# FFN output of a hybrid decoder block: 16 of its 22 contraction blocks as seven half-block products

## The chip, the cores and the metric

The kernel runs on one core of a Trainium2 chip. The metric is the device time of one execution in microseconds (us), median of the runs shown; lower is better. A separate profiled execution gives the trace. Engines are named as the profile names them: PE (TensorE matmuls), PEld (TensorE weight loads), DVE (VectorE), ACT (ScalarE), POOL (GpSimd) and SP (SyncE, which issues every DMA of this kernel).

## The reference, cut to what matters

One layer: an input projection, a Mamba-2 mixer and an RG-LRU mixer side by side, two output projections merged by gates, `w_out`, then the FFN that the change is about.

```python
h = h + (g_ssm * y_ssm + g_lru * y_lru) @ w_out[l]
hn = rmsnorm(h, norm2_w[l])
gate, up = jnp.split(hn @ w_ffn_in[l], 2, axis=-1)
h = h + (jax.nn.silu(gate) * up) @ w_ffn_out[l]
return rmsnorm(h, norm_f_w)
```

`h` is 1024 tokens by 1024 features; the FFN's hidden width is 2816 = 22 blocks of 128. All data is float32.

## The kernel before, in words

Everything is kept transposed: 128 features on the partitions, tokens along the free dimension, in two halves of 512 (`h`). A float32 operand is split into a high part `hi` (fp32r, a cast on ACT) and a low part `lo = x - hi` (a subtraction on DVE, with `x` and `hi` both in SBUF); `split`, lines 98 and 99. A product of two blocks is then three matmuls, hi·hi, lo·hi and hi·lo (lines 175 to 177 and 960 to 962). So each 128x128 weight block against 512 tokens costs three 128x512 matmuls, and each operand costs one ACT and one DVE instruction before it.

Stages in order: the input projection and the two mixers (to about 1000 us of the trace), the two mixer output projections, `w_out` (lines 965 to 1001), the FFN input (1008 to 1054), the FFN output (1057 to 1148). The tile framework places all semaphores and, from the order of the program and what is ready, the order on each engine; each engine runs its own queue in that order.

**The FFN input** already multiplies by halves. For a pair of column blocks (gate and up) and both token halves, the eight half-block products are replaced by seven, with sums of weight quarters made on POOL (`pair_sums`, four instructions of 512 columns) and sums of activation quarters made once, in the `w_out` stage (lines 988 to 999). One pair is 7 products of 12 matmuls, 84 matmuls; there are 22 pairs. The result of pair j is stored to the DRAM buffer `act_d[j]`.

**The FFN output** is direct: the 22 contraction blocks in four groups (`FFG`, of 6, 6, 5 and 5). For each of the first three groups the activations are loaded from `act_d` and split (`load_group`), and for each of 8 column tiles `d` and each token half a bank of PSUM collects the group's matmuls, and DVE adds it to `res` (line 1089). The last group runs over tokens 0 to 511, 512 to 767 and 768 to 1023, with the squares, the final norm and the stores of `out` folded in. Its weights come in through `last_w`, 512 columns at a time. At the change from the FFN input to the FFN output the pool `ar1` is closed and `ar2` and `res` are laid over its space.

PSUM has 8 banks of 512 columns (`pb`). SBUF tiles of two 512-column rows are "units", from the pools `ar0` (8) and `ar1` (29); `tp` has 13 tiles of 512 columns for short-lived values.

Of the kernel before, what the change touches and what calls it, by code (L numbers as in the profile page):

```python
# [60 lines left out]
NTMP = 13  # L61
NUNIT = 29

FFG = ((0, 6), (6, 12), (12, 17), (17, 22))
# [3 lines left out]
def hybrid_block(ctx, tc, xT, w_in, w_dt, w_os, w_ol, w_o, w_fi, w_fo, w_fl, lru_w, params, heads, out):  # L68
# [219 lines left out]
    with ExitStack() as st1:  # L288
# [470 lines left out]
        tp = ctx.enter_context(tc.tile_pool(name="tp", bufs=NTMP, reuse_waits="tile"))  # L759
# [3 lines left out]
        with tc.tile_pool(name="lru", bufs=1, reuse_waits="tile", side="right") as lp, tc.tile_pool(  # L763
# [66 lines left out]
            y0 = [act_pair(ar0, load_half(yn_d[i][:, hcol[0]])) for i in range(8)]  # L830
# [48 lines left out]
    yl = [load_acts(ar1, yl_d, h) for h in range(2)]  # L879
# [11 lines left out]
    for d in range(KD):  # L891
        mg[1][d] = act_pair(ar1, res[d][:, 1, :])
# [7 lines left out]

    raws, wops = {}, {}

    def pair_load(j):
        raws[j] = []
        for q in range(2):
            raw = wpool.tile([P, KD, P], F32, name="raw", tag="raw", bufs=2)
            load(raw, w_fi[q * NFF + j])
            raws[j].append(raw)

    def pair_a1(j):  # L910
        raw = raws[j][0]
        hi = wpool.tile([P, KD, P], F32R, name="whi", tag="whi")
        lo = wpool.tile([P, KD, P], F32R, name="wlo", tag="wlo")
        split(hi, lo, raw)
        wops[j] = {"a11": (hi[:, 0:4, :], lo[:, 0:4, :]), "a12": (hi[:, 4:8, :], lo[:, 4:8, :])}

    blk = lambda t_: t_.rearrange("p (k c) -> p k c", c=P)

    def pair_sums(j):

        g_, u_ = raws[j]
        s12, s34 = unit(ar1, F32, "s12"), unit(ar1, F32, "s34")
        s = [blk(t_[:, i, :]) for t_ in (s12, s34) for i in range(2)]
        G.tensor_tensor(s[0], u_[:, 0:4, :], u_[:, 4:8, :], op=ALU.add)
        G.tensor_tensor(s[1], s[0], g_[:, 0:4, :], op=ALU.add)
        G.tensor_tensor(s[2], g_[:, 0:4, :], u_[:, 0:4, :], op=ALU.add)
        G.tensor_tensor(s[3], s[1], g_[:, 4:8, :], op=ALU.add)
        wops[j]["s"] = s12, s34

    def pair_a22(j):  # L930
        u = unit(ar1, name="a22")
        hi, lo = blk(u[:, 0, :]), blk(u[:, 1, :])
        split(hi, lo, raws[j][1][:, 4:8, :])
        wops[j]["a22"] = hi, lo

    def pair_s(j, i):
        src = wops[j]["s"][i]
        hi, lo = unit(ar1, name="sh"), unit(ar1, name="sl")
        split(hi, lo, src)
        for q in range(2):  # L940
            wops[j][f"s{2 * i + q + 1}"] = blk(hi[:, q, :]), blk(lo[:, q, :])

    xop = {}

    def xop_put(name, k, pool, src, neg=False):

        if k % 2 == 0:
            xop.setdefault(name, []).append((unit(pool, name="xh"), unit(pool, name="xl")))
        hi, lo = (t_[:, k % 2, :] for t_ in xop[name][k // 2])
        if neg:  # L950
            S.activation(hi, src, AF.Copy, scale=-1.0)
            V.scalar_tensor_tensor(lo, src, -1.0, hi.bitcast(F32), op0=ALU.mult, op1=ALU.subtract)
        else:
            split(hi, lo, src)
# [12 lines left out]
    for h in range(2):
        for d in range(KD):
# [10 lines left out]
            sumsq(rs2[h], r, d == 0)  # L979
            k, kh = d % 4, d // 4  # L980
            if k % 2 == 0:
                bn[h, kh, k // 2] = unit(ar1, F32, "bn")
            b = lambda h_, kh_: bn[h_, kh_, k // 2][:, k % 2, :]
            S.activation(b(h, kh), r, AF.Copy, scale=pcol("n2", d))
            if h == 0:
                xop_put(("b11", "b21")[kh], k, ar1, b(h, kh))
            elif kh == 0:
                V.tensor_tensor(b(0, 0), b(1, 0), b(0, 0), op=ALU.subtract)
                xop_put("t1", k, ar1, b(0, 0))
            else:  # L990

                pool = ar0 if k < 2 else ar1
                V.tensor_tensor(b(0, 0), b(1, 1), b(0, 0), op=ALU.subtract)
                xop_put("t2", k, pool, b(0, 0))
                G.tensor_tensor(b(1, 0), b(1, 0), b(1, 1), op=ALU.subtract)
                V.tensor_tensor(b(0, 1), b(0, 1), b(0, 0), op=ALU.subtract)
                xop_put("t3", k, pool, b(1, 0))
                xop_put("t4", k, pool, b(0, 1))
                xop_put("n22", k, pool, b(1, 1), neg=True)
            if h == 1 and d == 0:  # L1000
                rms_scale(rs2[0], rs2[0], bank(), 1.0 / D, epst[:, 0:1])
    pair_sums(0)
    pair_s(0, 0)
    pair_a22(0)
    pair_s(0, 1)


    for j in range(NFF):
        wo = wops[j]
        last = j == NFF - 1  # L1010
        nxt = lambda f, *a: None if last else f(j + 1, *a)
        nxt(pair_load)
        px, pv, py, pz = bank(), bank(), None, None
        product(px, wo["a11"], "b11", True, False)
        s1 = temp("s1")
        S.copy(s1, px)
        if j == 0:
            product(px, wo["a12"], "b21", False, True)
            product(pv, wo["s1"], "t1", True, False)
        else:  # L1020
            product(pv, wo["s1"], "t1", True, False)
            product(px, wo["a12"], "b21", False, True)
        nxt(pair_a1)
        nxt(pair_sums)
        py = bank()
        product(py, wo["s2"], "t2", True, False)
        if j == 0:
            rms_scale(rs2[1], rs2[1], bank(), 1.0 / D, epst[:, 0:1])
        sg = temp("sg")
        V.tensor_tensor(sg, px, rs2[0], op=ALU.mult)  # L1030
        S.activation(sg, sg, AF.Silu)
        u2 = temp("u2")
        V.tensor_tensor(u2, s1, py, op=ALU.subtract)
        product(py, wo["s3"], "t3", False, True)
        nxt(pair_s, 0)
        V.tensor_tensor(s1, py, s1, op=ALU.subtract)
        su = temp("su")
        V.tensor_tensor(su, pv, s1, op=ALU.add)
        pz = bank()
        product(pz, wo["a22"], "t4", True, True)  # L1040
        nxt(pair_a22)
        V.tensor_tensor(s1, pz, s1, op=ALU.add)
        V.tensor_tensor(s1, s1, rs2[0], op=ALU.mult)
        V.tensor_tensor(sg, sg, s1, op=ALU.mult)
        store(act_d[j][:, hcol[0]], sg)
        product(pv, wo["s4"], "n22", False, True)
        nxt(pair_s, 1)
        V.tensor_tensor(u2, u2, pv, op=ALU.subtract)
        V.tensor_tensor(u2, u2, rs2[1], op=ALU.mult)
        S.activation(u2, u2, AF.Silu)  # L1050
        V.tensor_tensor(su, su, rs2[1], op=ALU.mult)
        V.tensor_tensor(u2, u2, su, op=ALU.mult)
        store(act_d[j][:, hcol[1]], u2)
        del wops[j], raws[j]
# [183 lines left out]
```

## Time and profile before

| what | value |
|---|---|
| three timed runs | 2108.53, 2112.59, 2111.17 us; median 2111.17 us |
| profiled execution | 2113.38 us, span of the trace 2111.4 us |
| PE busy | 2066.4 us, 9702 matmuls |
| DVE, ACT, POOL busy | 1261.3, 856.0, 406.7 us |
| granted TensorE clock, mean | 0.989 |
| DMA | 212.17 MB, 100 GB/s over the span |

Times in rows are microseconds from the start of the span unless marked ns. Matmuls are pipelined, so a matmul's own duration is longer than the distance from one to the next. "Idle before" is the time that an engine waited ahead of an instruction, with the instruction that ended the wait behind the arrow.

### The profile page before, as it was taken

To read this page: it belongs to the slowest core of one execution; us is meant where nothing else is said; L and a number is where in the kernel's file an instruction comes from. 1 tells how busy PE (TensorE), PEld (TensorE's weight loads), DVE (VectorE), ACT (ScalarE), POOL (GpSimd) and SP (SyncE) were. 2 spreads that over 40 slices of the span, in tenths; PEclk is the share of its full clock that TensorE was granted. 3 is DMA by queue.
4 is the path that set the end of the run, shared out by engine and by line. 5 is a ranking of instruction groups with operands and counts; after the bars stand their busy time and mean duration, and the time that the engine had idled before them with its cause. 6 is when DMAs were issued, how large, how long until landed. Compare 5 with 4: busy or idle time off the path is not lost.

```text
span 2111.4 us, 24842 instructions
## 1 busy us (share of the span) xinstructions
PE 2066.4 (98%) x9702; PEld 1681.2 (80%) x9702; DVE 1261.3 (60%) x1587; ACT 856.0 (41%) x1253; POOL 406.7 (19%) x378
## 2 busy tenths in 40 slices
PE   8999999999999999999999999988999999999998
PEld 6677887887887888888888888866888888878887
DVE  8655567567667546555514544588666666654336
ACT  5334445445455436666513221453223222233124
POOL 5103333334343410000000000234322332100000
PEclk8999999999999999999999999999999999999999
DMA  3222223323223243211314431542222222283122
GB/s 140 88 62 88 85 77 117 103 75 113 88 77 118 89 159 135 75 65 60 128 52 159 144 114 58 162 148 97 67 87 90 82 70 88 74 287 107 52 59 80
DMA packets 99973, 212.17 MB, mean 100 GB/s; under 512 B 11024, under 2 KB 29456, under 8 KB 99856
## 3 DMA queue, kind: packets, MB, share of 16 engines
q1 hardware_dynamic: 99856, 210.59, 30.9%
q8 instruction: 76, 1.25, 0.2%
q14 instruction: 41, 0.34, 0.1%
HBM read 168.34 MB, written 42.21 MB: 100 GB/s over the span
## 4 chain that ended last, share of the span: by engine, by line
PE 87%; DVE 5%; issue 2%; POOL 2%; ACT 2%; DMA 1%; SPq 0%; DVEq 0%; POOLq 0%; ACTq 0%
PE pj L175 12%; PE pj L177 11%; PE pj L176 11%; PE pbk L175 9%; PE pbk L177 9%; PE pbk L176 9%; PE pbk L960 6%; PE pbk L962 6%; PE pbk L961 6%; PE yb L661 1%; PE yb L649 1%; DVE xs L494 1%; PE tr L627 1%; DVE wlo L99 1%; DVE xl L332 1%
## 5 line engine op out<-in xcount | busy, mean ns | idle before, releaser
L175 PE MATMUL pj<-hnh,whi 128*128 128x512 f32 x1152 | 461.0, 400 | 0.0
L177 PE MATMUL pj<-hnl,whi 128*128 128x512 f32 x1152 | 452.8, 393 | 0.0
L176 PE MATMUL pj<-hnh,wlo 128*128 128x512 f32 x1152 | 451.7, 392 | 0.0
L177 PE MATMUL pbk<-un,whi 128*128 128x512 f32 x816 | 317.8, 390 | 1.3 <-DVE un L99 1.3
L175 PE MATMUL pbk<-un,whi 128*128 128x512 f32 x816 | 317.9, 390 | 1.0 <-ACT un L98 1.0
L176 PE MATMUL pbk<-un,wlo 128*128 128x512 f32 x816 | 317.3, 389 | 0.0
L98 ACT CAST whi<-raw 128x1024 fp32r<-128x1024 f32 (+3 forms) x172 | 167.2, 972 | 308.8 <-PE pbk L177 199.7
L99 DVE TENSOR_TENSOR wlo<-raw,whi 128x1024 fp32r<-128x1024 f32 (+3 forms) x172 | 201.5, 1172 | 142.8 <-ACT whi L98 140.9
L177 PEld LDWEIGHTS pj<-hnl,whi 128*128 128x128 f32 x1152 | 216.6, 188 | 48.1 <-issue 0.5
L175 PEld LDWEIGHTS pj<-hnh,whi 128*128 128x128 f32 x1152 | 216.7, 188 | 45.8 <-issue 2.4
L176 PEld LDWEIGHTS pj<-hnh,wlo 128*128 128x128 f32 x1152 | 216.9, 188 | 44.9 <-issue 1.4
L177 PEld LDWEIGHTS pbk<-un,whi 128*128 128x128 f32 x816 | 153.2, 188 | 35.2 <-DVE un L99 3.2
L175 PEld LDWEIGHTS pbk<-un,whi 128*128 128x128 f32 x816 | 153.2, 188 | 33.3 <-ACT un L98 1.7
L176 PEld LDWEIGHTS pbk<-un,wlo 128*128 128x128 f32 x816 | 153.2, 188 | 31.8 <-issue 0.2
L960 PE MATMUL pbk<-xh,sh 128*128 128x512 f32 x352 | 140.1, 399 | 13.2 <-ACT sh L98 10.0
L857 POOL TENSOR_TENSOR rs<-rs,sq 128x512 f32<-128x512 f32 x14 | 22.7, 1620 | 639.2 <-ACT sq L856 639.2
L961 PE MATMUL pbk<-xh,sl 128*128 128x512 f32 x352 | 137.3, 390 | 0.4 <-DVE sl L99 0.4
L962 PE MATMUL pbk<-xl,sh 128*128 128x512 f32 x352 | 137.3, 390 | 0.0
L620 ACT ACTIVATE E<-csb,cs 128x128 f32<-128x128 f32 x256 | 82.8, 392 | 107.6 <-PE yb L661 100.4
L98 ACT CAST sh<-s 128x1024 fp32r<-128x1024 f32 x44 | 46.3, 1052 | 171.3 <-PE pbk L961 157.8
L960 PEld LDWEIGHTS pbk<-xh,sh 128*128 128x128 f32 x352 | 66.1, 188 | 35.1 <-ACT sh L98 10.4
L1089 DVE TENSOR_TENSOR res<-res,pbk 128x512 f32<-128x512 f32 x48 | 32.8, 686 | 87.4 <-PE pbk L177 87.4
(265 smaller groups left out, 3366.3 us busy)
## 6 DMA issues: line engine op xcount, KB each, us to landing
raw<-in_w_in SPq DMA_DIRECT2D x74, 512.0 KB, 3.5
raw<-in_w_fi SPq DMA_DIRECT2D x44, 512.0 KB, 3.9
csb<-cs_d SPq DMA_DIRECT2D x64, 256.0 KB, 3.5
ld<-act_d SPq DMA_DIRECT2D x44, 256.0 KB, 5.4
yn_d<-xs SPq DMA_DIRECT2D x16, 512.0 KB, 3.2
ld<-yn_d SPq DMA_DIRECT2D x32, 256.0 KB, 5.2
raw<-in_w_os SPq DMA_DIRECT2D x16, 512.0 KB, 3.5
gt<-gate_d SPq DMA_DIRECT2D x32, 256.0 KB, 4.1
```

Of the source, the lines that this page charges most:

```text
L98: S.copy(hi, src)
L99: V.tensor_tensor(lo, src, hi.bitcast(F32), op=ALU.subtract)
L175: PE.matmul(ps, wh, xh, start=i == 0, stop=False)
L176: PE.matmul(ps, wl, xh, start=False, stop=False)
L177: PE.matmul(ps, wh, xl, start=False, stop=i == n - 1)
L332: V.scalar_tensor_tensor(lo, x, pcol("n1", k), hi.bitcast(F32), op0=ALU.mult, op1=ALU.subtract)
L620: S.activation(E[:, j, :], csb[:, j, :], AF.Relu, bias=cs[:, c, h0 + j : h0 + j + 1], scale=-1.0)
L857: G.tensor_tensor(acc, acc, sq, op=ALU.add)
L960: PE.matmul(ps, wh, xh, start=first and k == 0, stop=False, skip_group_check=True)
L961: PE.matmul(ps, wl, xh, start=False, stop=False, skip_group_check=True)
L962: PE.matmul(ps, wh, xl, start=False, stop=last and k == 3, skip_group_check=True)
L1089: V.tensor_tensor(r, r, ps, op=ALU.add)
```

## The change

The FFN output takes contraction blocks 0 to 15 in two parts of 8 (`NPART`), each by halves: the 8 blocks as two halves of 4 in the contraction, column tiles in pairs (p, p + 4) for p = 0 to 3, tokens in two halves. Eight half-block products become seven (`NQ`), each 4 blocks deep, 12 matmuls. It runs product by product over the four pairs of column tiles: 28 steps ("slots") of 12 matmuls in each part. Blocks 16 to 21 stay direct, in the last group (6 blocks in place of 5). A table of events, `at(slot, f, ...)`, says at which slot the loads, the sums and the splits are issued: loads 10 to 12 slots ahead, a weight split three slots ahead (`LAW`), an activation split in the four slots of the product before. The events ahead of slot 0 are issued between the products of the last FFN input pair (`lead`, `pump`).

The sums: weights, four POOL instructions for each p and part (`w_sum`); activations, one on DVE and three on POOL for each k of 0 to 3 and part (`x_diff`). Results go to `res` through one instruction a product (ACT for product 0, DVE reading PSUM for the others), and three POOL additions for each p and part.

The memory is laid out anew: `ar` has 22 units, `br` 6 (for `res`, `bn`, `c0`, `c1`, then `res` of the end), `sp1` five tiles of 512 columns, `wq` five units laid over `tp` when that is closed after the `w_out` stage; `tp` has 10 tiles. The FFN input keeps its seven products, but its operand sums are taken otherwise: the weight sums overwrite the raw weights in place, the activation sums (`t_parts`) are four DVE instructions and two splits of 1024 columns for each k, and the second token half of `w_out` runs over column tiles 4, 5, 6, 7, 0, 1, 2, 3. The stores of `out` go one column tile at a time, 24 in place of 12.

```diff
-NTMP = 13
-NUNIT = 29
-FFG = ((0, 6), (6, 12), (12, 17), (17, 22))
+NTMP = 10
+NUNIT = 22
+NPART = 2
+NLAST = NFF - 8 * NPART
...
+    wo_order = [list(range(KD)), [4, 5, 6, 7, 0, 1, 2, 3]]
+    wseq += [(w_o[d], KD) for h in range(2) for d in wo_order[h]]
...
+    def pair_sums(n):
+        g_, u_ = raws[n]
+        s1 = sp1.tile([P, H], F32, name="ws1", tag="ws1")
+        wops[n]["raw1"] = s1
+        G.tensor_tensor(blk(s1), u_[:, 0:4, :], u_[:, 4:8, :], op=ALU.add)
+        G.tensor_tensor(u_[:, 0:4, :], u_[:, 0:4, :], g_[:, 0:4, :], op=ALU.add)
+        G.tensor_tensor(g_[:, 0:4, :], g_[:, 0:4, :], blk(s1), op=ALU.add)
+        G.tensor_tensor(g_[:, 4:8, :], g_[:, 4:8, :], g_[:, 0:4, :], op=ALU.add)
...
+    def t_parts(x, k, u1, u2, pool):
+        V.tensor_tensor(u1[:, 0, :], u1[:, 0, :], u1[:, 1, :], op=ALU.subtract)
+        V.tensor_tensor(u1[:, 1, :], u1[:, 1, :], u2[:, 1, :], op=ALU.subtract)
+        V.tensor_tensor(u2[:, 1, :], u2[:, 1, :], u1[:, 0, :], op=ALU.add)
+        V.tensor_tensor(u2[:, 0, :], u2[:, 0, :], u2[:, 1, :], op=ALU.subtract)
+        for u, names in ((u1, ("t1", "t3")), (u2, ("t4", "t2"))):
+            hi, lo = unit(pool, name="xth"), unit(pool, name="xtl")
+            split(row(hi), row(lo), row(u))
...
-            if h == 1 and d == KD - 1:
+            if h == 1 and i == KD - 2:
                 pair_load(0)
-                pair_a1(0)
             ps = bank()
             mm_act(ps, w, mg[h])
+            if h == 1 and i == KD - 1:
+                pair_a1(0)
+                pair_sums(0)
+                pair_s1(0)
...
+    def first_pair():
+        product(px, wo["a11"], x["b11"], True, False)
+        S.copy(c1[:, 0, :], px)
+        product(px, wo["a12"], x["b21"], False, True)
+        product(pv, wo["s4"], x["b22"], True, True)
+        pair_s(0, 1)
...
+    LAW = 3
+    def x_part(i, n, k):
+        u1, u2 = xu[i, k], xu[i, k + 4]
+        src = (u1[:, 0], u2[:, 0], u1[:, 0], u2[:, 1], u2[:, 1], u1[:, 1], u2[:, 0])[n]
+        xop.setdefault((i, n), []).append(act_pair(ar, src))
+    def x_diff(i, k, n):
+        u1, u2 = xu[i, k], xu[i, k + 4]
+        if n == 0:
+            V.tensor_tensor(u1[:, 0], u1[:, 0], u1[:, 1], op=ALU.subtract)
+        elif n == 1:
+            G.tensor_tensor(u1[:, 1], u1[:, 1], u2[:, 1], op=ALU.subtract)
...
+    def w_sum(i, p, n):
+        g_, u_ = wr[i, p, 0], wr[i, p, 1]
+        if n == 0:
+            ws1[i, p] = blk(sp1.tile([P, H], F32, name="ws1", tag="ws1"))
+            G.tensor_tensor(ws1[i, p], u_[:, 0:4], u_[:, 4:8], op=ALU.add)
+        elif n == 1:
+            G.tensor_tensor(u_[:, 0:4], u_[:, 0:4], g_[:, 0:4], op=ALU.add)
+            G.tensor_tensor(g_[:, 0:4], g_[:, 0:4], ws1[i, p], op=ALU.add)
+        else:
+            G.tensor_tensor(g_[:, 4:8], g_[:, 4:8], g_[:, 0:4], op=ALU.add)
+    def w_part(i, n, p):
...
+        t_ = wpool.tile([P, 2, 4, P], F32R, name="wop", tag="whi" if (n * NP + p) % 2 else "wlo")
+        split(t_[:, 0], t_[:, 1], src)
...
+        for p in range(NP):
+            at(s0 - 12 + p, load_w, i, p, 0)
+            at(s0 - 6 + p, load_w, i, p, 1)
+            at(s0 - 10 + p, load_x, i, p)
+            at(s0 - 7 + p, load_x, i, p + 4)
+            at(s0 + p, w_sum, i, p, 0)
+            at(s0 + 3 + p, w_sum, i, p, 1)
+            at(s0 + 4 + p, w_sum, i, p, 2)
+            for n in range(NQ):
+                at(s0 + (n - 1) * NP + p, x_part, i, n, p)
+                at(s0 + n * NP + p - LAW, w_part, i, n, p)
+            at(s0 + 2 + p, x_diff, i, p, 0)
+            at(s0 + 9 + p, x_diff, i, p, 1)
+            at(s0 + 10 + p, x_diff, i, p, 2)
+            at(s0 + 15 + p, x_diff, i, p, 3)
...
+    def slot(i, n, p, banks):
...
+        product(ps, wop.pop((i, n, p)), xop[i, n], first, last)
...
+        elif n == 4:
+            V.tensor_tensor(r(0, 1), r(0, 1), ps, op=ALU.subtract)
+            G.tensor_tensor(r(0, 1), r(0, 1), s1, op=ALU.add)
+        elif n == 5:
+            V.tensor_tensor(s1, ps, s1, op=ALU.subtract)
+            G.tensor_tensor(r(1, 1), r(1, 1), s1, op=ALU.add)
+            G.tensor_tensor(r(1, 0), r(1, 0), s1, op=ALU.add)
...
+    for s in range(s_end):
+        run(s)
+        slot(s // (NP * NQ), s // NP % NQ, s % NP, banks)
...
+            if t0 == 0:
+                last_w(min(KD * nk // 4, (d + 2) * nk // 4 + 1))
+                if d >= 2:
+                    last_act(1, d - 2)
...
+            store(out[d, :, t0:t1], res[d][:, h, c])
```

## Rows read from the trace of the kernel before

**Rows 1.** The page, busy time and share of the span by engine.
```profile
PE 2066.4 (98%) x9702; PEld 1681.2 (80%) x9702; DVE 1261.3 (60%) x1587; ACT 856.0 (41%) x1253; POOL 406.7 (19%) x378
```

**Rows 2.** Windows by stage: length, PE, PEld, DVE, ACT, POOL busy, PEclk, DMA share, GB/s.
```profile
1305.00:1413.90 108.90, 108.90 (x481) 89.78 (x479) 69.84 (x74) 52.01 (x73) 23.36 (x14) 1.00 0.48 152
1413.90:1433.70 19.80, 8.27 (x26) 4.96 (x25) 18.88 (x17) 10.27 (x16) 12.81 (x8) 0.74 0.21 66
1433.70:1470.00 36.30, 33.07 (x145) 26.68 (x144) 29.21 (x31) 12.55 (x15) 16.05 (x12) 1.00 0.26 87
1470.00:1836.00 366.00, 366.00 (x1600) 297.81 (x1599) 246.15 (x286) 102.92 (x133) 104.02 (x73) 1.00 0.26 83
1856.00:1875.00 19.00, 17.00 (x68) 12.48 (x69) 11.59 (x18) 6.26 (x10) 0.00 (x0) 1.00 0.97 346
1875.00:2043.00 168.00, 168.00 (x743) 139.15 (x742) 74.06 (x106) 42.05 (x62) 0.00 (x0) 1.00 0.35 110
```

**Rows 3.** PE's waits over the whole span: who released it, total us, times, longest.
```profile
PE pbk L960 <- ACT sh L98: 10.0, 1, 10.0
```

**Rows 4.** Timeline of PE at the end of `w_out`: start, duration, instruction.
```profile
1411.59 0.39 PE L177 MATMUL pbk<-un,whi 128*128 128x512 f32 x1
...
1413.63 0.39 PE L177 MATMUL pbk<-un,whi 128*128 128x512 f32 x1
```

**Rows 5.** The chain that ended last: two FFN input pairs, 256-column matmuls, the end.
```profile
1809.10 0.60 PE pbk L960 x2
1828.34 0.60 PE pbk L960 x2
...
2099.97 0.12 PE pbk L177
...
2101.57 0.43 DVE res L1134
```

**Rows 6.** Timelines of the start of the FFN input, by engine.
```profile
1418.13 1.71 POOL L924 TENSOR_TENSOR s<-raw 128x512 f32<-128x512 f32 x1
...
1422.59 0.68 DVE L977 SCALAR_TENSOR_TENSOR r<-pbk,r 128x512 f32<-128x512 f32 x1
...
1431.34 0.58 ACT L1016 COPY s<-pbk 128x512 f32<-128x512 f32 x1
```

**Rows 7.** Timelines of POOL and DVE, end of a steady FFN input pair.
```profile
1715.88 1.30 POOL L925 TENSOR_TENSOR s<-s,raw 128x512 f32<-128x512 f32 x1
1717.95 1.44 POOL L926 TENSOR_TENSOR s<-raw 128x512 f32<-128x512 f32 x1 [0.78 <-PE pbk L962]
1719.35 1.74 POOL L927 TENSOR_TENSOR s<-s,raw 128x512 f32<-128x512 f32 x1
...
1718.87 1.07 DVE L1043 TENSOR_TENSOR s<-s,rs 128x512 f32<-128x512 f32 x1
1719.97 1.66 DVE L1044 TENSOR_TENSOR sg<-sg,s 128x512 f32<-128x512 f32 x1
1721.56 0.67 DVE L1048 TENSOR_TENSOR u<-u,pbk 128x512 f32<-128x512 f32 x1
```

**Rows 8.** Groups by line and shape, FFN stages: count, busy us, mean ns.
```profile
L1089 DVE TENSOR_TENSOR res<-res,pbk 128x512 f32<-128x512 f32 x48 | 32.8, 686 | 87.4 <-PE pbk L177 87.4
L99 DVE TENSOR_TENSOR un<-ld,un 128x512 fp32r<-128x512 f32 x44 | 28.1, 685 | 4.3 <-ACT un L98 4.3
...
L98 ACT CAST un<-ld 128x512 fp32r<-128x512 f32 x44 | 27.1, 622 | 15.5 <-DMA ld<-act_d 12.1 <-PE pbk L962 1.9
```

**Rows 9.** Timeline of DVE as the FFN output starts: six splits in a row.
```profile
1858.89 3.69 DVE L99 TENSOR_TENSOR un<-ld,un 128x512 fp32r<-128x512 f32 x6
```

**Rows 10.** The page, DMA issues: KB each, median us from issue to landing.
```profile
raw<-in_w_fi SPq DMA_DIRECT2D x44, 512.0 KB, 3.9
...
ld<-act_d SPq DMA_DIRECT2D x44, 256.0 KB, 5.4
```

More of the change, by code (lines that the diff above doesn't have):

```diff
@@ L827, in gate_done @@
                 return done
-            y0 = [act_pair(ar0, load_half(yn_d[i][:, hcol[0]])) for i in range(8)]
+            y0 = []
+            for i in range(8):
+                yr = sp1.tile([P, H], F32, name="ld", tag="ws1")
+                load(yr, yn_d[i][:, hcol[0]])
+                y0.append(act_pair(ar0, yr))
             for i in range(16 - last_gates, 16):
@@ L876, in hybrid_block @@
                     V.scalar_tensor_tensor(r, gt, 1.0, r, op0=ALU.add, op1=ALU.mult)
[L879 removed]
+    yl = [load_acts(ar, yl_d, h) for h in range(2)]
     mg = [[None] * KD for _ in range(2)]
@@ L910, in pair_a1 @@
-    def pair_a1(j):
-        raw = raws[j][0]
+            load(raw, w_fi[q * NFF + n])
+            raws[n].append(raw)
+    def pair_a1(n):
         hi = wpool.tile([P, KD, P], F32R, name="whi", tag="whi")
         lo = wpool.tile([P, KD, P], F32R, name="wlo", tag="wlo")
[L914 to L954, printed above, removed]
@@ L956, in product @@
-    def product(ps, w, x, first, last):
-        for k in range(4):
+        split(hi, lo, raws[n][0])
+        wops[n] = {"a11": (hi[:, 0:4, :], lo[:, 0:4, :]), "a12": (hi[:, 4:8, :], lo[:, 4:8, :])}
+    def pair_sums(n):
[6 more added lines that the diff above has]
+        G.tensor_tensor(g_[:, 4:8, :], g_[:, 4:8, :], g_[:, 0:4, :], op=ALU.add)
@@ new lines, in pair_s1, with pair_s, product @@
+    def pair_s1(n):
+        hi, lo = (sp1.tile([P, H], F32R, name=x, tag="ws1") for x in ("ws1h", "ws1l"))
+        split(hi, lo, wops[n].pop("raw1"))
+        wops[n]["s1"] = blk(hi), blk(lo)
+    def pair_s(n, q):
+        hi, lo = unit(wq, name="wsh"), unit(wq, name="wsl")
+        split(row(hi), row(lo), raws[n][q].rearrange("p k c -> p (k c)"))
+        for i, name in enumerate((("s2", "s4"), ("s3", "a22"))[q]):
+            wops[n][name] = blk(hi[:, i, :]), blk(lo[:, i, :])
+    def product(ps, w, xs, first, last):
+        n = len(xs)
+        for k in range(n):
@@ L1000, in hybrid_block @@
-            if h == 1 and d == 0:
+            sumsq(rs2[h], r, i == 0)
+            if h == 0:
+                bn[d] = unit(br if d not in (0, 4) else ar, F32, "bn")
+            b = bn[d][:, h, :]
+            S.activation(b, r, AF.Copy, scale=pcol("n2", d))
+            k = d % 4
+            if h == 0:
+                x2[("b11", "b21")[d // 4]][k] = act_pair(ar, b)
+            elif d >= 4:
+                x2["b22"][k] = act_pair(ar0, b)
+            else:
+                t_parts(x2, k, bn[k], bn[k + 4], ar0 if k == 0 else ar)
@@ L1001, in hybrid_block @@
+            if h == 1 and i == 0:
                 rms_scale(rs2[0], rs2[0], bank(), 1.0 / D, epst[:, 0:1])
-    pair_sums(0)
+    st_tp.close()
+    wq = ctx.enter_context(tc.tile_pool(name="wq", bufs=5, reuse_waits="tile", side="right"))
     pair_s(0, 0)
[L1004 to L1009, printed above, removed]
-        last = j == NFF - 1
[L1011 to L1054, printed above, removed]
@@ new lines, in hybrid_block, with at, run, load_res @@
+    NP, NQ = 4, 7
+    res = []
+    for d in range(KD):
+        res.append((lambda d=d: unit(br if d < 6 else (ar, ar0)[d - 6], F32, "res2")))
+    events = {}
+    def at(slot, f, *a):
+        events.setdefault(slot, []).append((f, a))
+    def run(slot):
+        for f, a in events.pop(slot, ()):
+            f(*a)
+    LAW = 3
+    xu, wr, wop, xop, s1u, ws1 = {}, {}, {}, {}, {}, {}
+    def load_res(d):
+        res[d] = res[d]()
+        load(row(res[d]), res_d[d])
+    def load_x(i, k):
+        pool = ar if i == 0 or k == 2 * NP - 1 else ar0
+        xu[i, k] = unit(pool, F32, "xu")
+        load(row(xu[i, k]), act_d[i * 8 + k])
@@ new lines, in hybrid_block @@
+    for d in range(KD):
+        at(d - 2, load_res, d)
+    for s in events:
+        events[s].sort(key=lambda e: e[0] in (load_x, load_w, load_res), reverse=True)
+    def slot(i, n, p, banks):
+        first, last = n in (0, 2, 4, 6), n in (1, 3, 5, 6)
+        if first:
+            banks[p] = bank()
+        ps = banks[p]
+        product(ps, wop.pop((i, n, p)), xop[i, n], first, last)
+        r = lambda q, h: res[q * 4 + p][:, h, :]
+        s1 = s1u[i, p] if n else None
+        if n == 0:
+            if p % 2 == 0:
+                s1u[i, p] = unit(wq, F32, "s1")
+                s1u[i, p + 1] = s1u[i, p][:, 1, :]
+                s1u[i, p] = s1u[i, p][:, 0, :]
+            S.copy(s1u[i, p], ps)
+        elif n == 1:
+            V.tensor_tensor(r(0, 0), r(0, 0), ps, op=ALU.add)
+        elif n == 2:
+            V.tensor_tensor(r(1, 1), r(1, 1), ps, op=ALU.subtract)
+        elif n == 3:
+            V.tensor_tensor(r(0, 1), r(0, 1), ps, op=ALU.add)
+        elif n == 4:
[5 more added lines that the diff above has]
+            G.tensor_tensor(r(1, 0), r(1, 0), s1, op=ALU.add)
+        else:
+            V.tensor_tensor(r(1, 0), r(1, 0), ps, op=ALU.add)
@@ L1068, in last_w, with lead @@
+    def lead():
+        for s in range(-12, 0):
+            run(s)
+            if s % 2:
+                yield
+    first_pair()
+    ahead_ = lead()
+    for j in range(1, NFF):
+        last = j == NFF - 1
+        pair(j, None if last else j + 1, (lambda: next(ahead_, None)) if last else lambda: None)
+    for _ in ahead_:
+        pass
+    wl, act = [], [[], []]
+    def last_w(n):
         for i in range(len(wl), n):
-            raw = wpool.tile([P, H], F32, name="raw", tag="raw", bufs=2)
+            raw = sp1.tile([P, H], F32, name="wl", tag="ws1")
@@ L1097, in hybrid_block, with last_act @@
-    nk = nl
-    act = acts[-1]
+            wl.append(act_pair(ar, raw))
+    def last_act(h, k):
+        raw = sp1.tile([P, H], F32, name="al", tag="ws1")
+        load(raw, act_d[8 * NPART + k][:, hcol[h]])
+        act[h].append(act_pair(ar0 if h == 0 or k < 2 else ar, raw))
+    s_end = NPART * NP * NQ
+    for k in range(NLAST):
+        at(s_end - 7 + k, last_act, 0, k)
+    for i in range(3):
+        at(s_end - 3 + i, last_w, i + 1)
+    banks = [None] * NP
+    for s in range(s_end):
+        run(s)
+        slot(s // (NP * NQ), s // NP % NQ, s % NP, banks)
```

200 lines of the change are left out of this document (119 added, 81 removed).

## The prediction, made before the change was run

> **What bounds the kernel now.** I read the busy shares first: PE is busy for 2066.4 of 2111.4 us and POOL for 406.7 [rows 1], so a saved matmul is worth its full time wherever PE runs without gaps. The windows by stage say where that is [rows 2]: `w_out` (108.90 of 108.90 us), the steady FFN input (366.00 of 366.00) and the FFN output from 1875 on (168.00 of 168.00). They also show two places where PE is not fed, the start of the FFN input (1413.9 to 1470) and the switch to the FFN output (1856 to 1875). PE's waits put one 10.0 us wait of an FFN input product at the first of these [rows 3].
>
> For the price of a matmul I take distances between starts, since the durations overlap: nine matmuls from 1411.59 to 1413.63 are 0.227 us each [rows 4]. In the FFN input by halves one pair takes 1828.34 - 1809.10 = 19.24 us for 84 matmuls, 0.229 us each; the 256-column matmuls of the end come 0.12 us apart [rows 5].
>
> **The arithmetic that goes.** Groups one to three of the FFN output are 17 blocks x 16 bank fills x 3 = 816 matmuls, 816 x 0.227 = 185.2 us. In their place stand 2 parts x 28 products x 12 = 672 matmuls. By halves I price them as in the FFN input: 672 x 0.229 = 153.9 us. Block 16 moves to the last group: 24 matmuls of 512 columns and 48 of 256, 24 x 0.227 + 48 x 0.12 = 11.2 us. Together 185.2 - 153.9 - 11.2 = 20.1 us less PE work. The FFN input keeps its 84 matmuls a pair.
>
> **The switch to the FFN output.** Between 1856 and 1875 some 68 matmuls run in 19.0 us [rows 2], 68 x 0.227 = 15.4: 3.6 us are lost while DMA is 97% busy at 346 GB/s. The change issues these loads during the last pair. What product 0 needs is four x tiles and one weight tile of 512 KB, but units come free only as the last pair's products release their operands: two at its start, four after its first product, four after its third. At 346 GB/s a tile takes about 1.5 us (512 KB / 346 GB/s), and the pair lasts 19.24 us, so twelve tiles can be in by its end; the splits of 4 x 0.69 us on DVE follow [rows 8]. Best 0 lost, worst 6 (four late tiles); I take 3, so 0.6 us is gained.
>
> **The start of the FFN input.** From 1413.9 to 1470 are 56.1 us with 26 + 145 matmuls [rows 2], 171 x 0.229 = 39.2, and two plain float32 matmuls of the norm add about 1.4: 15.5 us are lost. POOL begins the weight sums only at 1418.13, DVE takes the last residual at 1422.59, nine microseconds after its matmuls ended, and ACT copies the first product out of PSUM only at 1431.34 [rows 6]; the second product into that bank waits for the copy. The change issues the sums ahead of the last residual, so they can start when the second raw tile lands, some 6 us earlier, and `t_parts` has no POOL instruction. Against that, DVE's chain stays: for each k the residual, four differences and two splits of 1024 columns, 0.69 + 4 x 0.69 + 2 x 1.23 = 5.9 us [rows 8, 9] beside a weight split, against 24 x 0.227 = 5.4 us of matmuls, so DVE is still late when PE ends. And the raw tiles are now freed only by the last split (sums in place), which delays the loads for pair 1; a load takes 3.9 us [rows 10]. Best 12 us gained (PE waits for one split only), worst 2 lost; I take 6 gained, nearest to the 6 us by which the sums are earlier.
>
> **The operands of the seven products.** This is the price of the change. One part is 28 products, 28 x 12 x 0.229 = 76.9 us of PE. In that time ACT does 56 casts of 0.62 us and four copies, 37 us [rows 8]: hidden. DVE does 28 activation splits, 28 weight splits and 4 differences, 60 instructions with both inputs in SBUF, and 24 that read PSUM. Back to back they come 3.69 / 6 = 0.615 us apart [rows 9]: 84 x 0.615 = 51.7 us, hidden with 25 us to spare if nothing delays them. POOL does 16 weight sums, 12 differences and 12 additions to `res`, 40 x 1.30 = 52 us: hidden as well by itself.
>
> But the two delay each other. In a steady pair L925 takes 1.30 us alone; L927, with DVE's L1044 beside it, takes 1.74, and L1044 takes 1.66 in place of 0.69, ending 0.54 us after POOL's end; L1043 takes 1.07. L1048, which reads PSUM while POOL has just finished, takes 0.67 [rows 7]. So a POOL instruction costs DVE up to 0.97 us, when DVE has an SBUF instruction waiting, and nothing when it hasn't. The four POOL instructions of that pair cost it 0.97 + 0.38 = 1.35, 0.34 each, with such instructions on DVE for 38% of the pair (three splits of 1024 columns and six instructions of 512, twelve units x 0.615 = 7.4 of 19.24 us). In the new part they are 60 x 0.615 / 76.9 = 48%, so I scale 0.34 to 0.43: DVE 51.7 + 40 x 0.43 = 68.9 of 76.9 us, hidden on average. It is not even in time, though: by the event table 14 of 28 slots issue two or three POOL instructions, where DVE needs 3 x 0.615 + 2 x 0.43 to 3 x 0.615 + 2 x 0.97, 2.7 to 3.8 us in a slot of 2.75. The leads, three slots for weights but one for the last activation split of a product, take some of it. Bounds: nothing lost; or 1 us in each of 28 such slots, 27. I take 0.3 in each, 8 us.
>
> **Edits at nothing.** Smaller pools in the `w_out` stage (`tp` 10 for 13, 22 units for 29): DVE is busy 69.84 of 108.90 us there and PE has no gap [rows 2], which covers loads that come later; without the cover a late load costs 1 to 2 us. The event table's loads move the same bytes as before, at 110 GB/s of 346 shown [rows 2]. The tail: 15 loads of last weights and activations now run through five tiles beside the last group's first 32 us; at 5.4 us to land [rows 10] and about 1 us to split, four tiles carry 20 in 32 us. I add 1 us (0 to 4). The end after the last matmul (2101.57 on [rows 5]) has the same DVE work and eight smaller stores in place of four: 0.
>
> **Sum.** -20.1 - 0.6 - 6 + 8 + 1 = -17.7 us. The profiled execution took 2113.4 us (2.2 above the median): 2095.7, and 2094 on the scale of the median 2111.2.
>
> **Rivals.**
> *VectorE and GpSimd take strict turns* and become the bound. For it: rows 7, where neither moved while the other held. Then a part needs 60 x 0.69 + 40 x 1.30 = 93.4 us against 76.9, 16.5 late, 33 for both in place of my 8: 2094 + 25 = 2119, slower than before. It decides from 89 us of turns in a part on ((76.9 + (17.7 + 8) / 2), where the whole gain is gone. Against it: the DVE hold is shorter than its 0.69 us (L926 ends at 1719.39, L927 at 1721.09, 1.70 us apart with L1043 between them, which leaves 0.40 us beside POOL's 1.30), and 60 x 0.40 + 52 is 76.0, just under the 76.9 of PE. The Trainium skill (SBUF — State Buffer, section "SBUF: two separate sides") calls this an exclusive lock held for the whole instruction, taken by a DVE instruction with two SBUF inputs against a GpSimd one that reads SBUF; the rows agree on the blocking, and by that rule alone the time would be this rival's 2119. Chance 0.17.
> *The DMA queue blocks at the switch.* SP issues in order; the fourth weight tile needs a `wq` unit that is released only after the last pair's sixth product, 16.5 us in. If the x tiles stand behind it, product 0 starts after four tiles (6 us), 2 us to land and the splits (2.8), about 9 us late in place of 3: 2100. For it: nothing in the program lets a later load pass an earlier one in SP's queue; against: the order of that queue is made from what is expected to be ready, as other queues here are. Chance 0.13, still faster.
> *Everything is hidden* and the start of the FFN input loses only 4 us: -20.1 - 3.6 - 12 = -35.7, 2078. Against it: DVE is late there in any order. Chance 0.10.
> The forecast, 2094 with its own range 2085 to 2105: 0.60.
>
> **How the numbers follow.** 0.2% (4.2 us) is about what a measurement can tell: faster is under 2107, slower over 2115.4. Of the strict-turns case about 0.09 lies above that, 0.07 between, 0.01 below; of the other cases 0.02 is slower (all terms at their bad ends) and 0.03 the same. Faster 0.79, same 0.10, slower 0.11. The range leaves out the strict turns' upper half and the best case's lower half: 2079 to 2113.
>
> **What would show it.** 9702 - 816 + 672 + 72 = 9630 matmuls or close. Right: in the stage by halves PE near 12 matmuls per 2.75 us, DVE near 90% busy with SBUF instructions stretched to 1 to 1.7 us beside POOL; no wait over 3 us at the switch; the start of the FFN input losing 8 to 11 us. Wrong: 28 products taking 90 us or more, with PE waiting for DVE's `wop` or x splits; or one long PE wait ended by a load of `act_d`. DVE being starved by POOL for most of a part, or a wait that this trace doesn't have, would make the prediction wrong.

## The result, and the profile after

The kernel became slower: 2124.20 us, median of four runs (2122.83 to 2124.27), beside 2111.88 us for the kernel before (2108.53 to 2113.15). The ratio is 1.0059, 95% interval 1.0042 to 1.0077. The forecast was 2094, a gain, so the sign was wrong; the nearest of the stated times is that of the strict-turns rival (2119). The profiled execution has a span of 2122.5 us, 11.1 more than before.

The page's busy times after the change:

```profile
PE 2060.7 (97%) x9630; PEld 1668.6 (79%) x9630; DVE 1321.9 (62%) x1606; ACT 879.8 (41%) x1289; POOL 529.8 (25%) x454
```

The 72 matmuls are gone as counted (9702 in [rows 1]), but PE's share fell from 98% to 97%: PE waits more. The windows by stage say where (columns as in [rows 2]); the last two are the output stage cut in the middle of its time, and not its two parts of 28 products:

```profile
1413.90:1434.50 20.60, 12.50 (x44) 9.48 (x43) 20.57 (x18) 10.44 (x14) 11.33 (x6) 0.83 0.14 42
1434.50:1470.00 35.50, 35.50 (x153) 28.32 (x153) 28.57 (x31) 12.26 (x15) 12.18 (x8) 1.00 0.31 103
1470.00:1836.00 366.00, 366.00 (x1579) 294.92 (x1578) 217.60 (x243) 97.70 (x113) 104.56 (x76) 1.00 0.23 82
1836.00:1856.40 20.40, 20.40 (x89) 16.45 (x88) 11.62 (x15) 3.92 (x6) 5.41 (x4) 1.00 0.88 306
1856.40:1949.00 92.60, 78.53 (x316) 61.44 (x316) 91.87 (x89) 37.31 (x65) 69.86 (x43) 0.94 0.44 163
1949.00:2041.30 92.30, 85.09 (x358) 68.44 (x357) 76.86 (x89) 35.34 (x63) 55.95 (x35) 0.96 0.11 35
```

The output stage lasts from its first matmul at 1856.44 to the first of the last group at 2041.56, 185.1 us for 672 matmuls; its second part of 28 products starts at 1960.15, so the parts take 103.7 and 81.4 us. In the first of the two windows DVE is busy 91.87 of 92.60 us with only 89 instructions, POOL 69.86 us, and PE has 316 matmuls where 92.6 / 0.227 = 408 would fit. The steady FFN input is as full as before, but holds 1579 matmuls in the same 366 us where [rows 2] have 1600. PE's waits name the engine (columns as in [rows 3]):

```profile
PE pbk L952 <- DVE wop L100: 14.0, 9, 3.7
PE pbk L953 <- DVE un L100: 7.3, 4, 3.2
PE pbk L951 <- ACT c L1023: 7.2, 1, 7.2
```

The third is the start of the FFN input, 10.0 us before [rows 3]. The first two are new: PE waits 21.3 us for DVE's splits in the output stage. At 0.2267 us each the 672 matmuls need 152.3 us, so 32.8 are lost. Most of the other 11.5 is matmuls 0.34 to 0.43 us apart after some of these waits: behind the longest wait, which ends at 1955.29, they come 0.43 us apart, and the granted clock from 1955.9 to 1961.0 is 0.50, the lower of its two levels (1.2 GHz).

Why DVE is late can be read from the groups by line and shape (columns as in [rows 8]) and the timelines of the two engines, both after the change:

```profile
L100 DVE TENSOR_TENSOR un<-xu,un 128x512 fp32r<-128x512 f32 x56 | 67.4, 1236 | 0.4
L100 DVE TENSOR_TENSOR wop<-wr,wop 128x512 fp32r<-128x512 f32 x32 | 34.3, 1075 | 0.0
L100 DVE TENSOR_TENSOR wop<-raw,wop 128x512 fp32r<-128x512 f32 x16 | 16.1, 1014 | 2.5 <-ACT wop L99 2.4
L1133 DVE TENSOR_TENSOR xu<-xu 128x512 f32<-128x512 f32 x8 | 11.9, 1503 | 0.0
L100 DVE TENSOR_TENSOR wop<-ws,wop 128x512 fp32r<-128x512 f32 x8 | 8.8, 1099 | 0.0
...
L1135 POOL TENSOR_TENSOR xu<-xu 128x512 f32<-128x512 f32 x8 | 14.2, 1785 | 2.5 <-DVE xu L1133 2.5
```

```profile
1942.82 1.74 POOL L1206 TENSOR_TENSOR res<-res,s 128x512 f32<-128x512 f32 x1
1944.52 1.73 POOL L1207 TENSOR_TENSOR res<-res,s 128x512 f32<-128x512 f32 x1
1946.21 3.44 POOL L1135 TENSOR_TENSOR xu<-xu 128x512 f32<-128x512 f32 x2
...
1943.33 3.48 DVE L100 TENSOR_TENSOR un<-xu,un 128x512 fp32r<-128x512 f32 x2
1946.73 0.68 DVE L1205 TENSOR_TENSOR s<-pbk,s 128x512 f32<-128x512 f32 x1
1947.33 1.17 DVE L100 TENSOR_TENSOR wop<-wr,wop 128x512 fp32r<-128x512 f32 x1
```

A split of this shape took 685 ns before [rows 8] and takes 1236; the five DVE groups are all 120 instructions with two SBUF inputs, 138.5 / 120 = 1.154 us each. POOL starts an instruction every 1.69 us without a pause, and DVE gets one split out for each of them (3.48 us for two); the DVE instruction that reads PSUM (`s<-pbk,s`) keeps its 0.68 us in the middle of POOL's work. In the trace 75 of the stage's 80 POOL instructions have a DVE instruction with two SBUF inputs running beside them.

### The profile page after: what moved, and what is told of

It reads as the page before. It is cut to its first block, busy times and chain, and to the rows that moved or that the text cites. A ratio compares the mean times of both kernels' runs of the same rounds, so it can differ in the third digit from the quotient of the medians.

```text
span 2122.5 us, 24859 instructions
## 1 busy us (share of the span) xinstructions
PE 2060.7 (97%) x9630; PEld 1668.6 (79%) x9630; DVE 1321.9 (62%) x1606; ACT 879.8 (41%) x1289; POOL 529.8 (25%) x454
## 4 chain that ended last, share of the span: by engine, by line
PE 80%; DVE 11%; issue 3%; ACT 3%; DMA 2%; POOL 1%; SPq 1%; DVEq 0%; ACTq 0%
PE pj L175 11%; PE pj L177 11%; PE pj L176 11%; PE pbk L951 8%; PE pbk L952 8%; PE pbk L953 7%; PE pbk L176 6%; PE pbk L177 6%; PE pbk L175 6%; DVE un L100 2%; PE yb L661 1%; DVE wop L100 1%; DVE wlo L100 1%; PE yb L649 1%; DVE xs L494 1%
## 5 line engine op out<-in xcount | busy, mean ns | idle before, releaser
L100 DVE TENSOR_TENSOR wlo<-raw,whi 128x1024 fp32r<-128x1024 f32 (+2 forms) x148 | 182.9, 1237 | 138.2 <-ACT whi L99 137.3
L99 ACT CAST whi<-raw 128x1024 fp32r<-128x1024 f32 (+2 forms) x148 | 147.8, 999 | 201.4 <-PE pbk L177 103.3
L175 PE MATMUL pbk<-un,whi 128*128 128x512 f32 x544 | 212.3, 390 | 0.9 <-ACT un L99 0.9
L176 PE MATMUL pbk<-un,wlo 128*128 128x512 f32 x544 | 211.8, 389 | 0.3 <-DVE wlo L100 0.3
L177 PE MATMUL pbk<-un,whi 128*128 128x512 f32 x544 | 211.9, 390 | 0.0
L175 PEld LDWEIGHTS pbk<-un,whi 128*128 128x128 f32 x544 | 102.1, 188 | 22.9 <-ACT un L99 1.6
L177 PEld LDWEIGHTS pbk<-un,whi 128*128 128x128 f32 x544 | 102.1, 188 | 22.2 <-DVE un L100 1.1
L176 PEld LDWEIGHTS pbk<-un,wlo 128*128 128x128 f32 x544 | 102.1, 188 | 22.0 <-DVE wlo L100 0.7
L952 PE MATMUL pbk<-un,wop 128*128 128x512 f32 x224 | 91.5, 408 | 14.0 <-DVE wop L100 14.0
L953 PE MATMUL pbk<-xtl,wsh 128*128 128x512 f32 x264 | 104.5, 396 | 0.0
L952 PE MATMUL pbk<-xth,wsl 128*128 128x512 f32 x264 | 104.3, 395 | 0.0
L951 PE MATMUL pbk<-xth,wsh 128*128 128x512 f32 x264 | 103.8, 405 | 0.0
```

Source lines behind the costliest of these rows:

```text
L99: S.copy(hi, src)
L100: V.tensor_tensor(lo, src, hi.bitcast(F32), op=ALU.subtract)
L175: PE.matmul(ps, wh, xh, start=i == 0, stop=False)
L176: PE.matmul(ps, wl, xh, start=False, stop=False)
L177: PE.matmul(ps, wh, xl, start=False, stop=i == n - 1)
L953: PE.matmul(ps, wh, xl, start=False, stop=last and k == n - 1, skip_group_check=True)
```

## The experiments

Theory **"turns"**: a VectorE instruction with both inputs in SBUF and a GpSimd instruction that reads SBUF exclude each other. Rivals: **"order"**, the sums simply come too late for their products, and **"full"**, VectorE has too much work. Each kernel below starts from the changed one, unless the text says otherwise, and its median stands against 2124.

**GpSimd's 80 instructions left out, or moved to VectorE.** Two kernels:

```diff
 # without them: the 10 lines on G in x_diff, w_sum and slot(), as here
 # (ws1 is then a view of its first input)
-            G.tensor_tensor(u1[:, 1], u1[:, 1], u2[:, 1], op=ALU.subtract)
+            pass
 # moved: the same 10 lines
+            V.tensor_tensor(u1[:, 1], u1[:, 1], u2[:, 1], op=ALU.subtract)
```

> All 80 GpSimd instructions of the output stage (sums of activation halves, of weight halves, and the additions of kept products) are left out, so the output is not the reference's; products, splits, evacuations and transfers stay. After the change that stage lasted 185 us for 672 matmuls that need 152.3 at 0.2267 us. Theory 'turns' (VectorE instructions that read SBUF twice wait for GpSimd's): the un<-xu splits fall from 1236 to about 690 ns, the stage to 155 to 160 us, the time to 2095 to 2101. Theory 'order' (the sums come too late for the products that need them, and VectorE's long durations only follow): also 2095 to 2101, but the splits that do not depend on a sum, as those of the raw weight halves, are as long as they were. If the transfers at the switch were the cause, the first three products stay near 18 us and the time stays above 2110.

> The same 80 instructions, moved from GpSimd to VectorE, nothing left out. 'Turns': VectorE gets 80 x 0.615 = 49 us more work but loses its 56 us of blocked time; its splits fall to about 690 ns, the stage is between 160 and 172 us, the time 2099 to 2112. 'Order' or 'VectorE is simply full': VectorE was busy 91.9 of 92.7 us in the first part, 25 us more in each part make the stage longer, and the time is 2124 to 2160.

Without them: 2091.49 us (2091.00 to 2092.78), below the 2095 to 2101 that I expected. On VectorE: 2092.30 (2090.88 to 2095.93), 0.9911 of the kernel before (0.9898 to 0.9925). The groups and the windows of the second:

```profile
L100 DVE TENSOR_TENSOR un<-xu,un 128x512 fp32r<-128x512 f32 x56 | 38.0, 683 | 0.0
L100 DVE TENSOR_TENSOR wop<-wr,wop 128x512 fp32r<-128x512 f32 x32 | 21.9, 684 | 0.1
```

```profile
1857.70:1934.00 76.30, 75.84 (x335) 62.39 (x334) 75.89 (x126) 39.48 (x68) 0.00 (x0) 1.00 0.53 192
1934.00:2010.60 76.60, 76.60 (x340) 63.34 (x339) 76.03 (x127) 33.80 (x59) 0.00 (x0) 1.00 0.12 33
```

"Full" is out: in the first window VectorE needs 75.9 us for 126 instructions (0.602 each), where it needed 91.9 for 89. The stage lasts 153.1 us (1857.69 to 2010.81), where 672 matmuls at 0.2267 need 152.3: 0.8 us is lost, at the switch. In the first kernel the splits of raw weight halves, which depend on no sum, fall too, from 1075 to 689 ns (`wop<-wr,wop`); "order" had them stay long. The expectation, 2099 to 2112, was too high, for one reason in both runs: I had left a part of the loss at the switch to the transfers, and it was turns as well. VectorE has 0.4 to 0.6 us to spare in a window.

**Only the 32 weight sums on GpSimd.**

```diff
 # G -> V in x_diff and slot(); w_sum stays on G
-            G.tensor_tensor(r(0, 1), r(0, 1), s1, op=ALU.add)
+            V.tensor_tensor(r(0, 1), r(0, 1), s1, op=ALU.add)
```

> Only the 32 sums of weight halves stay on GpSimd; the 24 sums of activation halves and the 24 additions of kept products go to VectorE. 'Turns': the loss goes with the number of GpSimd instructions, 32 of 80 leave 0.4 of the 56 us of blocked VectorE time, 22 us, and the time is between that of all on VectorE and 2124, near 2112. 'VectorE is full': 48 x 0.615 = 30 us more work on it, slower than 2124.

2112.26 us (2109.53 to 2114.29), as "turns" had it, and the splits are in between:

```profile
L100 DVE TENSOR_TENSOR un<-xu,un 128x512 fp32r<-128x512 f32 x56 | 48.7, 892 | 0.7 <-ACT un L99 0.7
```

So the loss grows with the number of GpSimd instructions, but not in proportion: 0, 32, 80 of them give 2092, 2112, 2124, and 0.4 of the instructions make 20 of the 32 us. About half of these 20 falls on the first three products, beside the weight sums that stand there, and VectorE has 48 instructions more to do than in the changed kernel.

**What the GpSimd instruction reads.** Two kernels keep all 80 in their places, but let them read nothing, or one input:

```diff
-            G.tensor_tensor(u2[:, 1], u2[:, 1], u1[:, 0], op=ALU.add)
+            G.memset(u2[:, 1], 0.0)                                          # reads nothing
+            G.tensor_scalar(u2[:, 1], u2[:, 1], 1.0, None, op0=ALU.mult)     # reads one
```

> The change with its 80 GpSimd instructions at the same places, but each only fills its output with zeros and reads nothing, so the output is not the reference's. If GpSimd's reading of SBUF is what VectorE takes turns with, the un<-xu splits fall to 690 ns and the time to 2091 to 2095. If any access of GpSimd to SBUF, or its presence, is enough, they stay above 1000 ns as long as GpSimd is busy, and the time is 2110 to 2124.

> The same places, but each GpSimd instruction reads one input (times 1.0) instead of two, so the output is not the reference's. If only an instruction of two SBUF inputs on GpSimd blocks VectorE, the splits are 690 ns and the time is 2091 to 2095. If one input is enough, the splits stay above 1000 ns, and the time is 2105 to 2124, by how long GpSimd then takes.

Reading nothing: 2091.33 us (2090.55 to 2091.50). Reading one: 2103.64 us (2102.63 to 2105.89). Groups of the first and of the second kernel:

```profile
L100 DVE TENSOR_TENSOR un<-xu,un 128x512 fp32r<-128x512 f32 x56 | 37.4, 689 | 1.0 <-ACT un L99 0.7
...
L1135 POOL MEMSET xu<- 128x512 f32 x8 | 4.2, 528 | 2.2 <-DVE xu L1133 1.9
```

```profile
L100 DVE TENSOR_TENSOR un<-xu,un 128x512 fp32r<-128x512 f32 x56 | 42.4, 783 | 20.1 <-ACT un L99 19.6
...
L1135 POOL TENSOR_SCALAR xu<-xu 128x512 f32<-128x512 f32 x8 | 13.5, 1696 | 0.0
L1139 POOL TENSOR_SCALAR xu<-xu 128x512 f32<-128x512 f32 x8 | 13.1, 1652 | 0.0
```

The one-input kernel came out between the two readings, and is the useful one. GpSimd is as slow as in the changed kernel (L1139: 1652 beside 1680 ns), so its results come as late, but the split needs only 783 ns. That parts "turns" from "order". The 12 us from 2091.3 to 2103.6 come with slow GpSimd work: ScalarE's casts wait 22.2 us there for sums on GpSimd, and VectorE 19.6 for ScalarE (the group above). The 20.6 us from 2103.6 to 2124.2 come with VectorE being held: in the first window after the change it is idle for 0.7 us only, so it hardly waits for a sum there. The parting is not exact, since an instruction with one input also waits for fewer producers, and still holds VectorE a little. In the run that reads nothing the split takes 689 ns, as with GpSimd idle (687).

The fills are also shorter (0.53 us), so one may ask whether they merely meet VectorE less often. The traces answer it when VectorE's instructions with two SBUF inputs are sorted by whether a GpSimd instruction runs at the same time:

| GpSimd's 80 instructions read | VectorE's beside one, mean ns (count) | VectorE's otherwise | GpSimd's beside one of these | GpSimd's alone, most of them |
|---|---|---|---|---|
| two inputs (changed kernel) | 1445 (77) | 684 (50) | 1677 | 1295 |
| one input | 794 (100) | 686 (27) | 1643 | 1490 |
| nothing | 688 (58) | 690 (69) | 528 | 527 |

A fill costs VectorE nothing even where they overlap. By the Trainium skill (SBUF — State Buffer, section "Who interferes with whom") VectorE contends here only with a GpSimd instruction that reads SBUF; the run agrees. That page makes no difference between one input and two; here it is 794 against 1445 ns beside such an instruction.

**The steady pair of the FFN input.** The changed kernel's pair was longer than before, which no part of the prediction had. In the memory layout of the two programs the split weight sums had moved: `wsh` and `wsl` lie in `wq`, at an address that is 96 modulo 128, every other matmul operand of the stage at 32.

```diff
-    wq = ctx.enter_context(tc.tile_pool(name="wq", bufs=5, reuse_waits="tile", side="right"))
+    wq = ctx.enter_context(tc.tile_pool(name="wq", bufs=5, reuse_waits="tile"))
```

> Only the pool of the split sums of the FFN input's weights (wsh, wsl) moves, by 1.3 KB, from an address that is 96 modulo 128 to one that is 32 modulo 128. Steady pairs of the FFN input lasted 19.485 us after the change and 19.233 before. Theory 'alignment': products with these weights go from 0.2333 to 0.2300 us a matmul or less, the pair to 19.2 to 19.3, the time to 2118 to 2120. Theory 'high address': the pair stays at 19.45 to 19.5, the time at 2124. Neither touches the output stage, which stays at 185 us.

2117.89 us (2116.76 to 2119.06). PE's timeline in the changed kernel, then with the pool moved; first and last of 15 and of 13 matmuls:

```profile
1479.74 0.40 PE L952 MATMUL pbk<-xth,wsl 128*128 128x512 f32 x1
...
1483.01 0.40 PE L952 MATMUL pbk<-xth,wsl 128*128 128x512 f32 x1
```

```profile
1479.79 0.39 PE L951 MATMUL pbk<-xth,wsh 128*128 128x512 f32 x1
...
1482.51 0.39 PE L952 MATMUL pbk<-xth,wsl 128*128 128x512 f32 x1
```

3.27 / 14 = 0.2336 us from one matmul to the next, against 2.72 / 12 = 0.2267. The chain that ended last has one row for each pair; changed kernel, then moved pool:

```profile
1517.60 0.58 PE pbk L951 x2
...
1829.33 0.58 PE pbk L951 x2
```

```profile
1516.66 0.60 PE pbk L951 x2
...
1824.40 0.60 PE pbk L951 x2
```

Sixteen pairs: 311.73 / 16 = 19.48 us, and 307.74 / 16 = 19.23, which is the pair before the change (19.24 in [rows 5]). 48 of a pair's 84 matmuls have such weights, so on average one of them costs 0.25 / 48 = 0.005 us more. To tell the alignment from the place, two more kernels: both repairs together, and the same with 64 bytes put ahead of the pool.

```diff
+    gap = ctx.enter_context(tc.tile_pool(name="gap", bufs=1)).tile([P, 16], F32, name="gap")
+    V.memset(gap, 0.0)
     wq = ctx.enter_context(tc.tile_pool(name="wq", bufs=5, reuse_waits="tile"))
```

> Both repairs at once: the 80 instructions on VectorE, and the pool of the FFN input's split sums at an address that is 32 modulo 128. Alone they brought 2092.3 and 2117.9 us against 2124. If the two losses are separate they add: 21 pairs x 0.25 us = 5 us, to 2085 to 2088. If VectorE, which the FFN input's pairs need too, gave the shorter pair back at the switch, it stays at 2090 to 2093.

> The same as the run with both repairs, with a gap of 64 bytes put ahead of that pool, so that it starts at 96 modulo 128 again, 1.3 KB from where it was after the change. 'Alignment': the pair goes back to 19.45 to 19.55 us and the time to 2091 to 2094. 'The address or the neighbours, not the alignment': pair 19.25, time as with both repairs.

Both repairs: 2087.12 us (2085.55 to 2087.86), 0.9881 of the kernel before (0.9865 to 0.9898), the best version that was run, along with the last one below. With 64 bytes ahead: 2092.38 (2090.70 to 2093.29), and its chain shows the long pair again:

```profile
1518.59 0.58 PE pbk L951 x2
...
1830.32 0.58 PE pbk L951 x2
```

311.73 / 16 = 19.48. So it is the alignment: 64 bytes bring it back, at a place 1.3 KB from the first one.

**The start of the FFN input.** There VectorE is stretched by the weight sums too, and PE waits 7.2 us. If turns cost time there, moving those sums should pay.

```diff
 # pair_sums, four lines; in the second kernel sumsq's addition as well
-        G.tensor_tensor(blk(s1), u_[:, 0:4, :], u_[:, 4:8, :], op=ALU.add)
+        V.tensor_tensor(blk(s1), u_[:, 0:4, :], u_[:, 4:8, :], op=ALU.add)
```

> The run with both repairs (2087.1 us), and the four sums of weight halves of each of the 22 FFN-input pairs moved from GpSimd to VectorE too. In the steady pairs TensorE lost nothing with them on GpSimd, so there nothing is expected. At the start of the FFN input (first product 7.2 us late, VectorE's instructions there 1.75 to 2.30 us instead of 0.69 to 1.22 while GpSimd works) 'turns' frees some 5 us of VectorE and adds 4 x 0.69 us: 2 to 4 us faster, 2083 to 2085. If VectorE's queue is simply full there, the four sums come on top: 2087 to 2090.

> As the run before, and the additions of squares for the second norm (GpSimd, 1.3 to 2.3 us each) on VectorE as well, so that GpSimd reads nothing from the start of the FFN input to the end. 'Turns': VectorE's last long instructions there go, another 0 to 2 us, 2082 to 2085. 'Full': the additions come on VectorE's path, 2087 to 2090.

2090.06 us (2088.73 to 2090.18) and 2086.12 (2085.69 to 2089.79), against 2087.12: the first is 3 us slower, the second the same, and my expectation of a gain failed. From the first product of the FFN input to the third pair they take 52.1 and 50.8 us, the run with both repairs 49.5. PE's waits at the start in the first of them:

```profile
PE pbk L951 <- ACT wsh L99: 4.1, 1, 4.1
PE pbk L952 <- DVE wsl L100: 2.1, 1, 2.1
PE pbk L951 <- ACT c L1023: 1.8, 1, 1.8
```

The wait for the copy fell from 7.2 to 1.8 us, but 4.1 and 2.1 us for the next splits took its place: VectorE still has the residuals and operands to do, whoever does the weight sums. That this is why nothing was gained is argued from the waits, and no run takes that work away.

## Why the prediction was wrong

The step that failed is the one called the price of the change: "so I scale 0.34 to 0.43: DVE 51.7 + 40 x 0.43 = 68.9 of 76.9 us, hidden on average", and with it the 8 us. A GpSimd instruction cost VectorE 0.79 us on average, VectorE was busy for 84.4 us a part, and the stage was 20 us longer than forecast. Everything else together was off by 9 us.

- **The delay of VectorE by GpSimd, 8 us forecast; the whole stage 164.9 forecast (153.9 + 3 + 8), 185.1 measured, 20.2 too long.** In the first window VectorE was busy 91.87 us for 89 instructions of 0.602: 38.3 us of holding, over 43 GpSimd instructions 0.89 us each; in the second 76.86 - 53.6 = 23.3 over 35, 0.67; together 61.6 over 78, 0.79. I had the ceiling, 0.97, in [rows 7], and scaled down to 0.43 by the share of time in which VectorE has such an instruction. That share is not given from outside. Once an instruction is held, those behind it queue up, so the next GpSimd instruction meets a waiting one: 75 of the 80 did. The rival had this: turns as the bound, decided from 89 us a part; the two parts averaged 92.6. That its own 93.4 came so near is partly luck: the parts took 103.7 and 81.4 us, and a turn 1.69 us and not 1.30 + 0.69. Its "against" counted the turns alone (76.0 us a part), just under PE's time; but VectorE works in order, and its own queue was the longer one: 60 x 1.154 = 69.2 and 24 x 0.602 = 14.4 for those that read PSUM, 83.6 us a part where PE needs 76.2. The rest of the stage's time is what PE and DVE then lose by waiting for each other, and PE's slower clock behind its waits. The Trainium skill's exclusive lock (SBUF — State Buffer, section "SBUF: two separate sides") pointed the right way in its sign; its "whole instruction" is more than the timeline shows, where one of each takes 1.69 us and not 1.30 + 0.69.
- **The matmuls, -20.1.** Right, a little too small: with the sums on VectorE the stage took 153.1 us in place of 153.9.
- **The switch, 3 us taken.** About 10 us were lost in the first three products of the changed kernel, and 0.8 with the sums on VectorE and the same transfers. So the transfers were in time; here too it was GpSimd's work. The rival of a blocked DMA queue didn't happen.
- **The start of the FFN input, -6.** Right in size: from its first product to the third pair 56.6 us before (1413.86 to 1470.42), 50.7 after (1416.12 to 1466.78). Which of the reasons given carried it was not tested.
- **The smaller pools, put at nothing.** The changed kernel reaches the FFN input 2.3 us later, and 2.0 of them are lost at one place, in the mixer output projections, where the reason given (DVE's slack in `w_out`) did not look. ScalarE's casts wait 4.0 us there for loads of `yn_d`, which came in time before, and PE falls behind with them (its timeline after the change, below; before, these matmuls are 0.23 us apart). The prediction itself had priced a late load that no slack covers at 1 to 2 us. That the smaller pools are the reason is likely, but no run gave them their tiles back. With the pair as long as before (`wq` moved) the output stage begins at 1851.14, against 1855.08 before the change: 6.0 gained at the start of the FFN input, less 2.1.

```profile
1053.24 0.40 PE L177 MATMUL pbk<-un,whi 128*128 128x512 f32 x1
1054.53 0.50 PE L175 MATMUL pbk<-un,whi 128*128 128x512 f32 x1 [0.89 <-ACT un L99]
```

- **The FFN input's pairs, "keeps its 84 matmuls a pair", forecast at no change.** +0.25 us in each of 21 pairs, 5.3 us, by the alignment of one pool. No step had it: [rows 5] gave the price of a matmul, and I took it to hold wherever the operands lie.
- **The tail, +1.** From the end of the stage to the end of the span 80.9 us, where the forecast's terms make 79.7 (256.3 before from 1855.08 on, less 188.8, plus 11.2 and 1): 1.2 more. In the other kernels it is 78.9 to 81.1, so this says little.

20.2 + 2.1 + 5.3 + 1.2 = 28.8, which is the way from -17.7 to +11.1. With the sums on VectorE the span was 2090.3, 21.1 less than before; the forecast without its 8 us, and with the 5.3, makes -20.4.

What the prediction named as the sign of its being wrong was seen: 28 products taking 90 us or more, 103.7 in the first part, with PE waiting for `wop` and x splits. The chance of 0.17 for that was too low: the traces of before showed the mechanism itself, and only its frequency was in question. Two of the prediction's sums are a little off, and change nothing: the rival's bound comes to 89.8 us a part, not 89, and "everything is hidden" to 2076 on the scale of the median, not 2078.

Open: why one SBUF input on GpSimd holds VectorE so much less than two, and why weights at 96 modulo 128 cost 0.005 us a matmul. Other alignments, and the operand that streams, were not tried.

## What to carry to other kernels

Where two engines hold each other and the faster has little slack, cost every instruction of the slower one near the full price of a turn (here 0.79 of at most 0.97 us); an average over a stage with slack does not carry over. Work moved to an idle engine can cost more than it frees: VectorE did the 80 sums itself in 80 x 0.602 = 48 us, less than the 61.6 (38.3 + 23.3) for which it was held while GpSimd did them. When a change lays memory out anew, the price of an instruction that "stays the same" is to be checked again, and a repaired wait is only worth the distance to the next one.

## What the runs showed of the hardware

- A VectorE instruction with two SBUF inputs (128x512 float32) takes 683 to 690 ns with no GpSimd instruction or beside a fill, which reads nothing; 794 beside a GpSimd instruction with one input, and 1445 beside one with two. One that reads PSUM keeps 0.68 us beside them.
- GpSimd and VectorE in turn: one of each every 1.69 us (128x512 float32), where GpSimd's takes 1.30 alone and VectorE's come 0.60 us apart.
- Matmuls of 512 columns whose weights start at 96 modulo 128 bytes of a partition come 0.2336 us apart in the stretch shown, at 32 modulo 128 0.2267; on average over a pair the difference is 0.005 us.
